# A hybrid transformer block on one core: the low part of K as one zero-padded 128-row tile per key head

## The chip, the cores and the metric

The kernel runs on one core of one Trainium2 chip, as one program in one launch. The metric is the device time of that program in microseconds, from the first to the last instruction that the device runs. Smaller is better. Inputs, weights and constant tables come from the chip's memory; the output of the last layer goes back to it.

## The reference

Two layers of a block that mixes 512 tokens `x` (width 1024) with 256 context tokens `ctx`. In each layer three branches run side by side (attention, a Fourier mixer, a long convolution called Hyena), then an output projection, then a feed-forward part with a short convolution. What matters here is the attention:

```python
kc = rmsnorm(pc_kv[..., :KV_W].reshape(B, C, N_KV_HEADS, HEAD_DIM), g_k[i])
q = rope2d(rmsnorm(px[..., Q0:K0].reshape(B, L, N_Q_HEADS, HEAD_DIM), g_q[i]), ang_r, ang_c)
k = rope2d(rmsnorm(px[..., K0:V0].reshape(B, L, N_KV_HEADS, HEAD_DIM), g_k[i]), ang_r, ang_c)
k_all = jnp.concatenate([kc, k], axis=1)          # 256 + 512 = 768 keys
s = jnp.einsum('bqhgd,bkhd->bhgqk', q, k).astype(jnp.float32) * (HEAD_DIM ** -0.5)
p = jax.nn.softmax(s, axis=-1).astype(v.dtype)
attn_x = blocked_attention(q.reshape(B, L, N_KV_HEADS, GQA_GROUP, HEAD_DIM), k_all, v_all)
```

There are 8 query heads and 2 key heads of 64 channels, so 4 query heads share a key head. In the first layer the context attends to itself as well (256 queries, 256 keys); in the last layer only `x` is computed.

## The kernel before

All products must be as exact as float32, but TensorE is fed with a reduced float type (`F32R`). So every operand is split into a high and a low part of 12 bits each, and a product is a sum of several products of parts. For most products these are three matmuls (`mm3`, lines 196 to 198): high by high, high by low, low by high.

Scores do the same with the parts stacked on partitions. The operand `Q` of one query head is a tile of 128 partitions: 64 rows hold q's high part, the other 64 its low part. For heads of key head 0 the high part is in rows 0 to 63, for heads of key head 1 in rows 64 to 127. `KD_[kv]` ("KDup") holds K's high part twice, in both halves of the partitions; one matmul over 128 rows gives (q high + q low) by K high. The third term, q high by K low, comes from the tile `KL_` ("KLo"): one tile for both key heads, with K's low part of head 0 in rows 0 to 63 and of head 1 in rows 64 to 127. That matmul reads 64 rows of `Q` and 64 rows of `KLo` (the slice `k64`), and adds to the same PSUM range.

A score tile is 128 queries by 768 keys, in a PSUM tile `pw` (there are two). It is written in two ranges of 512 and 256 columns, each with a product of KDup and a product of KLo, in this order: KDup 512 (line 966), KLo 512 (967), KDup 256 (966), KLo 256 (967). Then VectorE takes the negative maximum of each row (`nmax`, line 969), ScalarE the exponential into a tile `p` (973). There are 8 heads by 4 tiles of queries, so 32 score tiles in a layer, 64 in all. `attention` runs them ahead of the rest: a head has six steps, one for each 128 keys. A step transposes four blocks of `p` on TensorE (1018), splits the result into `pT` (ScalarE copies the high part, line 181; VectorE subtracts, line 182), and multiplies `pT` with V two steps later (1005). The first four of a head's six steps also issue a score tile of the next head. After the sixth step follow the sums of the exponentials, spread over partitions by eight small matmuls (1010), and the scaling (1090 to 1092). `attention_small` does the same for the context in the first layer, with score tiles of 256 columns (1050 and 1051), two for each of 8 heads.

KDup and KLo are filled by `post_k`: for each 128 keys a transpose (620), then copies of 64 partitions out of PSUM, two into KDup (ScalarE line 624, VectorE 625) and one into KLo (ScalarE, 626).

Tiles with the tag `M` (128 x 1024 float32 each) share 27 buffers; KDup, KLo, V, Q, p, pT, the normed operands `h` and most others are of this kind. A tile gets a buffer that is free, and its first writer waits for the last reader of the buffer's tile before.

The order of the work on each engine is not that of the code. A scheduler in the framework plays the program on a model of the engines, gives out buffers, and writes one queue for each engine; each queue is then run in its order. Beside the main line of code there are fillers (generators that are pumped while the main line would wait). SyncE's queue issues most loads, and GpSimd's (POOL) some: tables for the transforms (`dft`, `fd`), and the spilled operand `h` of the context (line 451).

Of the kernel before, what the change touches and what calls it, by code (L numbers as in the profile page):

```python
# [15 lines left out]
DRAM = bass.MemoryType.DRAM  # L16

P = 128
# [6 lines left out]
NKV = 2  # L25
# [10 lines left out]
# columns of the per-channel pack  # L36
# [9 lines left out]
def f32(ap):  # L46
    return ap.bitcast(F32)
# [6 lines left out]
# weights of products in the order of emission  # L54
# [14 lines left out]
class Net:  # L69
# [13 lines left out]
    # ---- order of emission: a main line, and fillers for the times in which it waits  # L83
# [48 lines left out]
    def go(self, name, gen, bg=0.0):  # L132
        """the main line; bg: share of fillers run beside it"""
        self.phase(name, gen)
        owed = 0.0
        for c, w in gen:
            self.now += c
            if w > 0:
                self.pump(w)
            owed += c * bg  # L140
            while owed > 0:
                f = self.ready()
                if f is None:
                    break
                t = self.now
                self.step(f)
                owed -= max(self.now - t, 0.05)
                self.now = t
            owed = min(owed, 1.0)
            self.phase(name, gen)  # L150

    # ---- tiles
# [25 lines left out]
    # ---- exact split into two parts of 12 bits  # L178
# [21 lines left out]
    # ---- 1/sqrt(sum / n + eps) of sums of n squares, by Newton steps; n a power of 4  # L200
# [18 lines left out]
    def rstd(self, ss):  # L219
        """1/sqrt of a mean square from the sums of two halves: the root, its inverse, and a Newton step"""  # L220
# [20 lines left out]
    # ---- constants  # L241
# [28 lines left out]
    # ---- modulation: block b (512 columns) of layer l  # L270
# [20 lines left out]
    def mod_chan(self, l, which, out, ahead=None):  # L291
        """which 0: norm before the mixer, 1: before the FFN."""
# [39 lines left out]
    # ---- norm of a token-major tile, transposed to channels on partitions, modulated, split  # L332
    def norm_diag(self, x, n):
        """the scale of a token on a diagonal, to be applied by the transposing product; n: where the result goes"""
# [8 lines left out]
    def turn(self, ps, n, b):  # L343
        """a half of a token tile, channels on partitions"""
# [26 lines left out]
    def norm_tile(self, st, t, n, AB, el=None, dve=4):  # L371
# [4 lines left out]
        if t == 0:  # L376
            # by 256 tokens, so that the first half of them can be read before the rest is written
# [20 lines left out]
    def norm_tile7(self, st, t, n, AB):  # L398
        """the seven left operands of Winograd's form, by halves of the tokens and of the channels"""
# [41 lines left out]
    def keep_h(self, st):  # L441
        """the operands of the next layer, kept in DRAM"""
# [19 lines left out]
    # ---- token-major products of 128 tokens with 512 columns of weights  # L462
    def proj_acc(self, st, name, l, h, tok_ap, ncol=512, early=0, late=None, w=None):
        """all the token tiles at once, by 256 of the contracted channels"""
# [28 lines left out]
    # ---- q: norm per head, RoPE, split, transposed  # L493
# [19 lines left out]
    def head_norm_rope(self, raw, nh, rstd, e, t, rope):  # L513
        """raw [P, nh, 64] -> normed, gained (and rotated) tile [P, nh, 64]"""
# [59 lines left out]
    # ---- k, v and the Fourier branch's input; tokens in the order even, odd  # L574
    def alloc_kv(self):
        self.KD_ = [self.M("KDup")[:, :768] for _ in range(NKV)]
        self.KL_ = self.M("KLo")[:, :768]
# [31 lines left out]
    def post_k(self, st, kraw, kss, kt0):  # L609
# [3 lines left out]
        for t in range(st.NT):  # L613
# [9 lines left out]
            for h in range(NKV):  # L623
                nc.scalar.copy(self.KD_[h][0:64, cs], pv[0:64, h])
                nc.vector.tensor_copy(self.KD_[h][64:128, cs], pv[0:64, h])
                nc.scalar.copy(self.KL_[64 * h : 64 * h + 64, cs], pv[64:128, h])
            yield 2 * CTR, 0.0

    # ---- Hyena branch: projection in channel-major form, short convolution
# [7 lines left out]
    def proj_hyena(self, l, st, late=None, parts=None, w=None):  # L637
# [32 lines left out]
        if late:  # L670
            # two at a time, by halves of the tokens as they become ready
# [23 lines left out]
    # ---- implicit filter and its spectrum, by even and odd taps  # L695
# [13 lines left out]
    def dft(self, key, st, a, ft):  # L709
        """two DFT matrices for one tile of frequencies, each (hi, lo)"""  # L710
# [58 lines left out]
    def filter_spectrum(self, l, st, keep, o):  # L769
# [3 lines left out]
        for ft in range(half):  # L773
            Kt = self.M("K", F32).rearrange("p (s q d) -> p s q d", s=2, q=2)
            for s in range(2):
# [4 lines left out]
                # Kt[:, s, 0]: at k; Kt[:, s, 1]: at T - k; s: cosine, sine part  # L780
                nc.vector.tensor_tensor(Kt[:, s, 0, :], eo[:, 0], eo[:, 1], op=ALU.add)
                nc.gpsimd.tensor_tensor(Kt[:, s, 1, :], eo[:, s], eo[:, 1 - s], op=ALU.subtract)
                if ft == 0 and s == 1:
                    # row 0 holds k = 0 and k = T; k = T / 2 apart
# [22 lines left out]
    # ---- Hyena branch: long convolution  # L807
    def hyena(self, l, st, keep):
# [50 lines left out]
        for ft in range(nf):  # L859
# [7 lines left out]
            # folded: [:, 0, 0] even cos, [:, 0, 1] odd cos, [:, 1, 0] even sin, [:, 1, 1] odd sin  # L867
# [29 lines left out]
    # ---- Fourier branch  # L897
# [56 lines left out]
    # ---- attention  # L954
    def scores(self, st, h, t):
# [8 lines left out]
        k64 = slice(64 * kv, 64 * kv + 64)  # L964
        for a, b in segs:
            nc.tensor.matmul(ps[:, a:b], Q[:, qs], self.KD_[kv][:, a:b], start=True, stop=False)
            nc.tensor.matmul(ps[:, a:b], Q[k64, qs], self.KL_[k64, a:b], start=False, stop=True)  # L967
# [65 lines left out]
    def attention_small(self, st):  # L1033
        """256 keys and queries: a head's scores, transposes and products in three steps"""
# [5 lines left out]
        for i in range(NH + 2):  # L1040
            c = 0.0
            if i < NH:
                kv = i // g
                k64 = slice(64 * kv, 64 * kv + 64)
# [3 lines left out]
                for t in range(NT):  # L1048
                    qs = slice(t * P, (t + 1) * P)
                    nc.tensor.matmul(sc[:, t], Q[:, qs], self.KD_[kv][:, 0:T], start=True, stop=False)  # L1050
                    nc.tensor.matmul(sc[:, t], Q[k64, qs], self.KL_[k64, 0:T], start=False, stop=True)
# [48 lines left out]
    # ---- residual update of a token-major tile: src + rstd * (y * G), in place of y * G  # L1100
# [13 lines left out]
    def mix_out(self, l, st, src, dst, nxt=None):  # L1114
        """output projection, then the residual update tile by tile"""
# [48 lines left out]
    def ffn_down(self, l, st, g, ms, begin, el=None, early=0, mid=None):  # L1164
        """the products of a group with w_down, added to y; after the last one, the residual update"""
# [41 lines left out]
    def ffn_c(self, l):  # L1207
        """the tokens of the context"""
        nc, st = self.nc, self.Cx
        G = 2  # L1210
# [29 lines left out]
    def ffn_x(self, l):  # L1240
        """the tokens of x alone; the first product by Winograd's form of Strassen's seven products"""
# [339 lines left out]
def _shape_constants():  # L1581
# [3 lines left out]
    for name, T in (("x", L), ("c", C)):  # L1585
# [3 lines left out]
        # Hyena: transform of length 2T, taps by parity  # L1589
# [12 lines left out]
        # [which, tile of frequencies, p, hi/lo, ...]  # L1602
        c[f"hdft_{name}"] = np.stack([tiles(m).reshape(P, 2, R, R, P).transpose(3, 0, 1, 2, 4) for m in fwd]).reshape(2, 2, R, P, 2, R, P).transpose(0, 2, 3, 1, 4, 5, 6)
        c[f"hinv_{name}"] = np.stack([tiles(fwd[j].T).transpose(2, 0, 1, 3) for j in (0, 2, 1, 3)]).reshape(2, 2, R, P, 2, H).transpose(0, 2, 3, 1, 4, 5)
        # Fourier: transform of length T, tokens by parity
# [7 lines left out]
        # Hyena filter: positions and windows  # L1613
# [41 lines left out]
def _layout(i):  # L1655
# [7 lines left out]
    # [l, block, half of its columns and of the contracted channels, p, 4, 256]  # L1663
# [37 lines left out]
```

## Time and profile before

| what | value |
|---|---|
| median of three runs | 1848.1 us (1838.39 to 1848.52) |
| span of the profiled execution, first to last instruction | 1850.3 us |
| mean granted TensorE clock in the profile | 0.952 |
| TensorE matmuls | 1718.8 us busy (93%), 10502 of them |
| TensorE weight loads | 1423.2 us (77%) |
| VectorE | 1446.4 us (78%) |
| ScalarE | 933.0 us (50%) |
| GpSimd | 693.4 us (37%) |
| mean DMA rate | 134 GB/s |

The profile gives no other time of its execution than this span; it is 2.2 us longer than the median of the runs. "Busy" is the time in which a row of that engine is under way; matmuls overlap, so two rows in succession can each be longer than the distance of their starts. PE is TensorE's matmul side, PEld its weight loads, DVE VectorE, ACT ScalarE, POOL GpSimd. A granted clock of 1.00 is full speed. In a row of the timeline the first column is the start in us, the second the duration in us; a merged row (x4) counts from the first start to the last end. In brackets stand the idle time before and what ended it.

### The profile page before, as it was taken

To read this page: it belongs to the slowest core of one execution; us is meant where nothing else is said; L and a number is where in the kernel's file an instruction comes from. 1 tells how busy PE (TensorE), PEld (TensorE's weight loads), DVE (VectorE), ACT (ScalarE), POOL (GpSimd) and SP (SyncE) were. 2 spreads that over 40 slices of the span, in tenths; PEclk is the share of its full clock that TensorE was granted. 3 is DMA by queue.
4 is the path that set the end of the run, shared out by engine and by line. 5 is a ranking of instruction groups with operands and counts; after the bars stand their busy time and mean duration, and the time that the engine had idled before them with its cause. 6 is when DMAs were issued, how large, how long until landed. Compare 5 with 4: busy or idle time off the path is not lost. (4 is left out here: it accounts for less than half of the span.)

```text
span 1850.3 us, 27827 instructions
## 1 busy us (share of the span) xinstructions
PE 1718.8 (93%) x10502; PEld 1423.2 (77%) x10502; DVE 1446.4 (78%) x2324; ACT 933.0 (50%) x1737; POOL 693.4 (37%) x511
## 2 busy tenths in 40 slices
PE   5899988999999998999999997998999789999997
PEld 2677865667788897878989886786678678989996
DVE  5789777567576689889898988486675976999997
ACT  2633344456574454556555556335563454545554
POOL 3344231000032447665554646021001446555552
PEclk9899999889999998999999999997799789999999
DMA  9224368500577652332342367542002253232322
GB/s 370 92 61 147 106 216 286 178 1 25 192 243 247 215 176 77 103 114 81 103 140 89 105 232 284 206 127 80 0 15 89 96 167 114 81 114 92 115 69 114
DMA packets 70002, 248.00 MB, mean 134 GB/s; under 512 B 8111, under 2 KB 9647, under 8 KB 69868
## 3 DMA queue, kind: packets, MB, share of 16 engines
q1 hardware_dynamic: 60716, 215.54, 34.4%
q0 software_dynamic: 9152, 30.68, 5.3%
q8 instruction: 83, 1.36, 0.3%
q14 instruction: 51, 0.42, 0.1%
HBM read 232.03 MB, written 14.16 MB: 133 GB/s over the span
## 5 line engine op out<-in xcount | busy, mean ns | idle before, releaser
L196 PE MATMUL pn<-h,Wh 128*128 128x256 f32 x1328 | 378.0, 287 | 8.0 <-ACT h L181 2.3
L198 PE MATMUL pn<-h,Wl 128*128 128x256 f32 x1328 | 374.3, 285 | 11.1 <-DVE Wl L182 11.1
L197 PE MATMUL pn<-h,Wh 128*128 128x256 f32 x1328 | 375.8, 284 | 1.9 <-POOL h L182 1.9
L196 PEld LDWEIGHTS pn<-h,Wh 128*128 128x128 f32 x1328 | 254.9, 193 | 20.2 <-issue 4.3
L198 PEld LDWEIGHTS pn<-h,Wl 128*128 128x128 f32 x1328 | 253.6, 192 | 16.0 <-DVE Wl L182 13.4
L197 PEld LDWEIGHTS pn<-h,Wh 128*128 128x128 f32 x1328 | 255.4, 192 | 6.3 <-POOL h L182 2.1
L181 ACT CAST Wh<-Wr 128x1024 fp32r<-128x1024 f32 x118 | 122.7, 1049 | 136.2 <-PE pn L197 46.5
L1275 POOL TENSOR_TENSOR tt<-r,r 128x512 f32<-128x512 f32 x44 | 75.9, 1724 | 270.7 <-DMA r<-w_up 243.4
L182 DVE TENSOR_TENSOR Wl<-Wr,Wh 128x1024 fp32r<-128x1024 f32 x89 | 130.3, 1472 | 50.8 <-ACT Wh L181 43.5
L196 PE MATMUL pw<-Wh,gT 128*128 128x512 f32 x352 | 137.1, 402 | 8.8 <-ACT gT L181 3.9
L197 PE MATMUL pw<-Wl,gT 128*128 128x512 f32 x352 | 138.6, 397 | 1.9 <-DVE Wl L182 1.9
L198 PE MATMUL pw<-Wh,gT 128*128 128x512 f32 x352 | 138.3, 398 | 1.8 <-DVE gT L182 1.8
L181 ACT CAST Wh<-tt 128x1024 fp32r<-128x1024 f32 x88 | 90.8, 1048 | 85.8 <-PE pn L197 43.6
L182 DVE TENSOR_TENSOR Wl<-tt,Wh 128x1024 fp32r<-128x1024 f32 x88 | 122.4, 1410 | 11.3 <-ACT Wh L181 8.4
L1334 POOL TENSOR_TENSOR ft<-ft,ft 128x512 f32<-128x512 f32 x44 | 70.6, 1603 | 133.9 <-DVE ft L635 90.7
L182 POOL TENSOR_TENSOR h<-tf,h 128x256 fp32r<-128x256 f32 (+1 forms) x40 | 38.0, 967 | 215.6 <-ACT h L181 214.2
L1201 DVE TENSOR_TENSOR y<-y,pw 128x1024 f32<-128x1024 f32 x82 | 99.3, 1214 | 22.0 <-PE pw L198 21.9
L969 DVE TENSOR_REDUCE nmax<-pw 128x1 f32<-128x768 f32 x64 | 61.1, 957 | 58.5 <-PE pw L967 58.5
L182 POOL TENSOR_TENSOR Wl<-Wr,Wh 128x1024 fp32r<-128x1024 f32 x29 | 73.1, 2526 | 58.4 <-ACT Wh L181 57.8
L1277 POOL TENSOR_TENSOR tt<-r,tt 128x512 f32<-128x512 f32 x44 | 74.8, 1699 | 50.8 <-DVE Wl L182 50.8
L181 ACT CAST pT<-pn 128x512 fp32r<-128x512 f32 x104 | 60.2, 585 | 64.2 <-PE pn L1018 61.9
L196 PE MATMUL pw<-h,Wh 128*128 128x256 f32 (+1 forms) x224 | 77.9, 348 | 12.4 <-ACT h L181 3.1
(360 smaller groups left out, 4795.7 us busy)
## 6 DMA issues: line engine op xcount, KB each, us to landing
wm<-w_mod SPq DMA_DIRECT2D x96, 512.0 KB, 5.3
r<-w_up SPq DMA_DIRECT2D x90, 512.0 KB, 3.6
Wr<-w_down SPq DMA_DIRECT2D x66, 512.0 KB, 3.7
L<-w_up SPq DMA_DIRECT2D x44, 512.0 KB, 4.6
Wr<-w_out SPq DMA_DIRECT2D x24, 512.0 KB, 3.5
Wr<-w_in_t SPq DMA_DIRECT2D x16, 512.0 KB, 4.2
dft<-hdft_x POOLq DMA_DIRECT2D x16, 512.0 KB, 4.4
Wr<-w_in_c SPq DMA_DIRECT2D x12, 512.0 KB, 3.4
```

What stands on the lines that cost most here:

```text
L181: r = nc.scalar.copy(hi, src)
L182: (el or nc.vector).tensor_tensor(lo, src, f32(hi), op=ALU.subtract)
L196: nc.tensor.matmul(ps, l[0], r[0], start=first, stop=False, **kw)
L197: nc.tensor.matmul(ps, l[0], r[1], start=False, stop=False, **kw)
L198: nc.tensor.matmul(ps, l[1], r[0], start=False, stop=last, **kw)
L969: nc.vector.tensor_reduce(nm, ps[:, :NK], axis=AX.X, op=ALU.max, negate=True)
L1201: nc.vector.tensor_tensor(y, y, acc[t], op=ALU.add)
L1275: te.tensor_tensor(half(t13, 0), half(r[1], 0), half(r[0], 0), op=ALU.subtract)
L1277: te.tensor_tensor(half(t24, 0), half(r[1], 1), half(t13, 0), op=ALU.subtract)
L1334: nc.gpsimd.tensor_tensor(o[0], o[0], o[1], op=ALU.mult)
```

## The change

Each key head gets a KLo tile of its own, of all 128 partitions. K's low part stands in 64 of its rows, where it meets q's high part; the other 64 rows, which meet q's low part, are set to zero by GpSimd when the tiles are allocated. The product with KLo then takes all 128 rows of `Q` and of `KLo`, so it has the same shape as the product with KDup. Further hunks of the diff only take comment lines out.

```diff
     def alloc_kv(self):
         self.KD_ = [self.M("KDup")[:, :768] for _ in range(NKV)]
-        self.KL_ = self.M("KLo")[:, :768]
+        self.KL_ = [self.M("KLo")[:, :768] for _ in range(NKV)]
+        for h in range(NKV):
+
+            self.nc.gpsimd.memset(f32(self.KL_[h][64 - 64 * h : 128 - 64 * h]), 0.0)
         self.V_ = [self.M("V")[:, :768].rearrange("p (t c) -> p t c", c=P) for _ in range(NKV)]
...
                 nc.vector.tensor_copy(self.KD_[h][64:128, cs], pv[0:64, h])
-                nc.scalar.copy(self.KL_[64 * h : 64 * h + 64, cs], pv[64:128, h])
+                nc.scalar.copy(self.KL_[h][64 * h : 64 * h + 64, cs], pv[64:128, h])
...
-        k64 = slice(64 * kv, 64 * kv + 64)
         for a, b in segs:
             nc.tensor.matmul(ps[:, a:b], Q[:, qs], self.KD_[kv][:, a:b], start=True, stop=False)
-            nc.tensor.matmul(ps[:, a:b], Q[k64, qs], self.KL_[k64, a:b], start=False, stop=True)
+            nc.tensor.matmul(ps[:, a:b], Q[:, qs], self.KL_[kv][:, a:b], start=False, stop=True)
...
-                k64 = slice(64 * kv, 64 * kv + 64)
...
                     nc.tensor.matmul(sc[:, t], Q[:, qs], self.KD_[kv][:, 0:T], start=True, stop=False)
-                    nc.tensor.matmul(sc[:, t], Q[k64, qs], self.KL_[k64, 0:T], start=False, stop=True)
+                    nc.tensor.matmul(sc[:, t], Q[:, qs], self.KL_[kv][:, 0:T], start=False, stop=True)
```

The scheduler places the new instructions, and some others move. Lines of the changed kernel are 3 higher behind `alloc_kv`, then 2, then 1.

GpSimd's queue in the first layer, where the context's keys are about to be projected. `fsd` and `taps` belong to the implicit filter of the Hyena branch, `fd` is a table of the Fourier branch. Before:

```order
L754 TENSOR_TENSOR fsd_1690<-dec_1687 128x256
L922 DMA fd_1869<-fdft_c 128x512
L754 TENSOR_TENSOR fsd_1750<-dec_1745 128x256
L751 TENSOR_TENSOR taps_1318<-taps_1318,fab_1747 128x512
L754 TENSOR_TENSOR fsd_1836<-dec_1831 128x256
```

The same place of the changed kernel:

```order
L757 TENSOR_TENSOR fsd_1693<-dec_1690 128x256
L580 MEMSET KLo_1654 64x768
L580 MEMSET KLo_1655 64x768
L925 DMA fd_1872<-fdft_c 128x512
L757 TENSOR_TENSOR fsd_1753<-dec_1748 128x256
L754 TENSOR_TENSOR taps_1318<-taps_1318,fab_1750 128x512
```

Two memsets of 64 rows by 768 columns stand ahead of a table's load; the work behind them keeps its order.

GpSimd's queue at the end of the first layer, where the context's operand `h` is fetched for the second layer's keys. `ft` is a gate of the feed-forward part, `y` its result. Before:

```order
L1334 TENSOR_TENSOR ft_10788<-ft_10788,ft_10789 128x512
L1334 TENSOR_TENSOR ft_10899<-ft_10899,ft_10900 128x512
L451 DMA h_10920<-spill_h 128x1024
L451 DMA h_10921<-spill_h 128x1024
L451 DMA h_10922<-spill_h 128x1024
L451 DMA h_10923<-spill_h 128x1024
L1197 TENSOR_TENSOR y_7559<-y_7559,G_5542 128x512
```

The same place of the changed kernel:

```order
L1335 TENSOR_TENSOR ft_10791<-ft_10791,ft_10792 128x512
L1335 TENSOR_TENSOR ft_10902<-ft_10902,ft_10903 128x512
L580 MEMSET KLo_10920 64x768
L580 MEMSET KLo_10921 64x768
L451 DMA h_10926<-spill_h 128x1024
L451 DMA h_10927<-spill_h 128x1024
L451 DMA h_10928<-spill_h 128x1024
L451 DMA h_10929<-spill_h 128x1024
L1198 TENSOR_TENSOR y_7562<-y_7562,G_5545 128x512
```

The memsets stand ahead of the four loads of `h`.

TensorE's queue in the first head of the first layer's attention, at a step that issues a score tile. Before:

```order
L1005 MATMUL pn_3464<-pT_3417,V_1655 128x512 x2
L1018 MATMUL pn_3467<-ident,p_3371 128x128
L1018 MATMUL pn_3467<-ident,p_3381 128x128
L1018 MATMUL pn_3467<-ident,p_3390 128x128
L1018 MATMUL pn_3467<-ident,p_3399 128x128
L966 MATMUL pw_3454<-KDup_1652,Q_951 128x512
L967 MATMUL pw_3454<-KLo_1654,Q_951 128x512
L966 MATMUL pw_3454<-KDup_1652,Q_951 128x256
L967 MATMUL pw_3454<-KLo_1654,Q_951 128x256
```

The same place of the changed kernel:

```order
L1007 MATMUL pn_3467<-pT_3420,V_1658 128x512 x2
L1020 MATMUL pn_3470<-ident,p_3374 128x128
L968 MATMUL pw_3457<-KDup_1652,Q_951 128x512
L969 MATMUL pw_3457<-KLo_1654,Q_951 128x512
L968 MATMUL pw_3457<-KDup_1652,Q_951 128x256
L969 MATMUL pw_3457<-KLo_1654,Q_951 128x256
L1020 MATMUL pn_3470<-ident,p_3384 128x128
L1020 MATMUL pn_3470<-ident,p_3393 128x128
L1020 MATMUL pn_3470<-ident,p_3402 128x128
```

Three transposes moved behind the score tile; apart from this the queue of the two attentions of `x` keeps its order, as it does on VectorE and ScalarE. Outside, the queues differ mainly in two stretches: around the first layer's projections of K and V, and from the end of the first layer's feed-forward part to the second layer's attention. There whole runs of matmuls of two accumulation groups are interleaved in another way.

## Prediction

> **What bounds the kernel now.** I read the page first (which engine is full), then the change's own lines, then the timeline around them, then busy time and granted clock by stretches.
>
> ```profile
> PE 1718.8 (93%) x10502; PEld 1423.2 (77%) x10502; DVE 1446.4 (78%) x2324; ACT 933.0 (50%) x1737; POOL 693.4 (37%) x511
> ```
>
> TensorE is the engine to look at, but 93% is an average, and overlapping rows count as busy while the array may be waiting. The products that the change touches:
>
> ```profile
> L967 PE MATMUL pw<-KLo,Q x128: 379/492/792, 316.8 to 1380.0; 64*128 64x512 f32 x64, 64*128 64x256 f32 x64
> L1051 PE MATMUL pn<-KLo,Q x16: 378/380/385, 246.0 to 302.4; 64*128 64x256 f32 x16
> ```
>
> They are 144 of 10502 matmuls. "64*128 64x512" says that they contract over 64 rows. What they cost shows in the distance of starts. First a stream of full-height products of 512 and 256 columns, then one whole score tile:
>
> ```profile
> 341.50 0.28 PE L196 MATMUL pn<-dft,Yh 128*128 128x256 f32 x1
> 341.62 0.28 PE L197 MATMUL pn<-dft,Yh 128*128 128x256 f32 x1
> ...
> 347.12 0.39 PE L196 MATMUL pn<-Wh,mx 128*128 128x512 f32 x1
> 347.36 0.40 PE L197 MATMUL pn<-Wl,mx 128*128 128x512 f32 x1
> ...
> 349.20 0.50 PE L966 MATMUL pw<-KDup,Q 128*128 128x512 f32 x1
> 349.63 0.49 PE L967 MATMUL pw<-KLo,Q 64*128 64x512 f32 x1
> 350.06 0.39 PE L966 MATMUL pw<-KDup,Q 128*128 128x256 f32 x1
> 350.37 0.38 PE L967 MATMUL pw<-KLo,Q 64*128 64x256 f32 x1
> 350.68 0.55 PE L1018 MATMUL pn<-ident,p 128*128 128x128 f32 x3
> ```
>
> In the stream a product of 512 columns takes 0.235 us from start to start (347.12 to 347.36) and one of 256 takes 0.12. In the score tile they take 0.43 and 0.31, whichever height they have. The whole tile takes 350.68 - 349.20 = 1.48 us, where 2 x 0.235 + 2 x 0.12 = 0.71 would do. The weight loads show the reason:
>
> ```profile
> 347.36 0.19 PEld L198 LDWEIGHTS pn<-Wh,mx 128*128 128x128 f32 x1
> ...
> 349.63 0.18 PEld L967 LDWEIGHTS pw<-KLo,Q 64*128 64x128 f32 x1 [0.24 <-issue]
> ```
>
> Between products of one height, the load for the next starts beside the running matmul (347.36, under the matmul of L197). Between heights it starts only with its own matmul (349.63), after an idle time that nothing but issue explains: 0.19 us more for each of the four products. So a score tile has four changes of height at about 0.19 us.
>
> Is TensorE what the attention waits for? By stretches (us, then busy time of PE, PEld, DVE, ACT, POOL, clock, DMA share, GB/s):
>
> ```profile
> 380.00:384.00 4.00, 4.00 (x11) 0.50 0.00 0
> 384.00:388.00 4.00, 4.00 (x19) 0.78 0.00 0
> ...
> 388.00:446.00 58.00, 58.00 (x287) 40.15 (x287) 43.51 (x63) 36.35 (x72) 0.00 (x0) 1.00 0.00 1
> ...
> 1284.00:1316.00 32.00, 32.00 (x77) 19.02 (x77) 12.84 (x18) 11.39 (x25) 0.00 (x0) 0.50 0.00 0
> ```
>
> (The first two show PE alone.) In the attention of `x` no transfer runs, GpSimd is idle, VectorE is busy three quarters of the time, TensorE without a gap. It is TensorE's stage. And its first head runs at **half the granted clock**, about 32 us in each layer.
>
> **Part 1: the first head, at half clock.**
>
> ```profile
> 353.73 0.79 PE L966 MATMUL pw<-KDup,Q 128*128 128x512 f32 x1 [2.50 <-ACT p L973]
> ...
> 375.27 0.78 PE L966 MATMUL pw<-KDup,Q 128*128 128x512 f32 x1
> ...
> 377.72 1.22 PE L1005 MATMUL pn<-pT,V 128*128 128x512 f32 x2
> 378.74 1.05 PE L1018 MATMUL pn<-ident,p 128*128 128x128 f32 x4
> 379.44 0.78 PE L966 MATMUL pw<-KDup,Q 128*128 128x512 f32 x1
> ...
> 385.97 0.47 PE L966 MATMUL pw<-KDup,Q 128*128 128x512 f32 x1
> ...
> 1283.29 0.79 PE L966 MATMUL pw<-KDup,Q 128*128 128x512 f32 x1 [2.31 <-ACT p L973]
> ...
> 1318.18 0.48 PE L966 MATMUL pw<-KDup,Q 128*128 128x512 f32 x1
> ```
>
> TensorE first waits 2.5 us for an exponential, whose own delay lies on ScalarE; that wait stays, so 353.73 and 1283.29 stay, and I expect the clock to fall as before. Then a step takes 379.44 - 375.27 = 4.17 us: score tile 2.45, two products with V 1.02, four transposes 0.70. At half clock the score tile without changes of height takes 2 x 0.71 = 1.42, the step 3.14.
>
> Before the steps come score tiles alone, four in layer 0 and five in layer 1, over two PSUM buffers. There the ring counts: score, maximum, exponential, then the buffer is free.
>
> ```profile
> L969 DVE TENSOR_REDUCE nmax<-pw x64: 935/958/959, 319.2 to 1380.5; 128x1 f32<-128x768 f32 x64
> ...
> L973 ACT ACTIVATE p<-pw,nmax x64: 891/902/911, 341.9 to 1381.6; 128x768 f32<-128x768 f32 x64
> L973 ACT ACTIVATION_READ_ACCUMULATOR p<-pw,nmax x64: 192/201/205, 342.7 to 1382.4; 128x1 f32 x64
> ...
> L182 DVE TENSOR_TENSOR pT<-pn,pT x29: 676/691/693, 389.0 to 443.9; 128x512 fp32r<-128x512 f32 x29
> ```
>
> (1.42 + 0.96 + 1.10) / 2 = 1.74 us a tile. Layer 0: 353.73 + 4 x 1.74 + 1.72 (V and transposes) = 362.4 for the fifth tile. Then four steps and the tail, which takes 385.97 - (379.44 + 2.45) = 4.1 now.
>
> Does the clock come back earlier? Now it returns only at about 386, behind a tail in which no score tile stands. In a step now, array work (1.42 + two products 0.94 + four transposes of some 0.5, an estimate from the rows above) fills 2.9 of 4.17 us, 69%; after the change 2.9 of 3.14, over 90%, which is like the tail. So I take it to return after one step. Layer 0: 362.4 + 3.14 + 3 steps at 2.0 (VectorE needs 0.96 + 0.69 in each, TensorE 1.5) + a tail of 2.2 = 373.8, **12.2 us** earlier. Layer 1 by the same sum: 1283.29 + 5 x 1.74 + 1.72 + 3.14 + 6.0 + 2.2 = 1305.0, **13.2 us** earlier. Should it stay at half for the whole head: 362.4 + 4 x 3.14 + 4.1 = 379.1 (6.9 us), and in layer 1 by the same sum 7.8 us.
>
> [...]
>
> **Part 2: five heads at full clock.**
>
> ```profile
> 397.27 1.05 PE L1010 MATMUL pn<-ident,den 128*128 128x128 f32 x8
> ...
> 445.87 1.05 PE L1010 MATMUL pn<-ident,den 128*128 128x128 f32 x8
> ...
> 453.75 1.05 PE L1010 MATMUL pn<-ident,den 128*128 128x128 f32 x8
> ...
> 458.91 1.05 PE L1010 MATMUL pn<-ident,den 128*128 128x128 f32 x8
> ```
>
> Line 1010 closes a head: (445.87 - 397.27) / 4 = 12.15 us each. Four score tiles give back 4 x 0.77 = 3.1, so TensorE needs 9.05. VectorE is then as late: 43.51 us in 58 is 9.1 a head. The last head, without score tiles, takes 458.91 - 453.75 = 5.16, below its VectorE rows (eight of 0.69 are 5.5, overlapping at the ends), so such a stage can run at VectorE's pace. With two equal engines and two PSUM buffers I take 9.6. That is 2.55 x 5 = 12.7, and 0.7 for one more tile: **13.4 us** a layer. Bounds: 3.1 a head (16.2 a layer) if no engine waits for another; 1.0 (5.4) if the ring of two buffers takes the rest.
>
> **Part 3: the context's attention.** 16 products of 256 columns, and 16 of KDup beside them, each 0.31 where 0.12 would do: 16 x 0.38 = 6.1 us at most; that stretch is shared with fillers that wait for transfers, so nothing at least. I take 2.
>
> **Part 4: memsets, buffers, order.** 64 rows by 768 columns on GpSimd is not in the trace. From below it may cost next to nothing; from above I take the row of 512 columns with two inputs, 1.5 times: 1.9 us.
>
> ```profile
> 195.59 0.58 POOL L922 DMA_DIRECT2D fd<-fdft_c  x1 [6.56 <-DVE dec L747]
> 196.20 0.75 POOL L754 TENSOR_TENSOR fsd<-dec 128x256 f32<-128x256 f32 x1
> 196.90 1.29 POOL L751 TENSOR_TENSOR taps<-taps,fab 128x512 f32<-128x512 f32 x1
> ...
> 1100.43 2.18 POOL L451 DMA_DIRECT2D h<-spill_h  x4
> ...
> L196 PE MATMUL pw<-M,h x16: 278/338/415, 1130.6 to 1143.2; 128*128 128x256 f32 x16
> ```
>
> In layer 0 two memsets (up to 3.9 us) fall into 6.56 us in which GpSimd waited. In layer 1 they hold the four loads of `h`, issued from 1100.43 and read from 1130.6: hidden by that distance. I take 0; uncovered it would be 4 us a layer. The second KLo tile takes one of 27 buffers until its head's keys are done; the queues of the attention kept their order, and the buffers that its p and pT tiles wait for were last read about as many instructions ahead as before. I take 0. The new interleaving outside the attention may give or take; waits there are short, so 6 us either way is my estimate, and 0 the value.
>
> **Sum.** 12.2 + 13.2 + 2 x 13.4 + 2 = 54 us. The profiled span, 1850.3, lies 2.2 above the median of the runs, and the profile shows no more of its time around it; the saving goes off the median: 1848 - 54 = **1794 us**.
>
> **Rivals.**
> 1. *The clock stays at half through the first head.* For: in the old trace 32 us of gapless rows did not raise it. Against: 69% of array work then, over 90% now. 6.9 + 7.8 + 26.8 + 2 = 44: **1804**.
> 2. *The two PSUM buffers take back most of Part 2* (1.0 a head), with or without Part 1's clock, and the new order costs 6: 25.4 + 10.8 - 6 = 30, or 20: **1818 to 1828**. For: VectorE and TensorE become equal. Against: the last head.
> 3. *The stall isn't from the height.* The idle would be there between any two products that share Q as weights and add to one PSUM range. Then nothing is saved: **1848**. Against: L966 after L1005 or L1018 has it only where heights change, and the products of a stream also add to one range. [...]
> [...]
>
> **How the numbers follow.** Forecast 54%, rival 1 26%, rival 2 10%, rival 3 7%, rival 4 3%. Low end: Part 2 at its full 16.2 a layer, Part 3 at 6, order 6: 25 + 32 + 6 + 6 = 69, 1779. High end: rival 2's 1828, so 10% is left out. One per cent (18 us) is about what a measurement of this kernel tells from no change. Faster by more than that: forecast, rival 1, rival 2 (its end is at the edge): 0.89; within 1%: 0.08; slower: 0.03.
>
> **What would show it.** Right: rows of KLo read 128*128; a score tile from start to start 0.71 at full clock; heads of 9 to 10 us; VectorE near 95% there; granted clock 1.00 from about 366 and 1297. Rival 1: clock 0.50 up to the first row of 1010. Rival 3: 0.43 between full-height scores. Wrong altogether: a row of `p` or `pT` that waits for buffers, a wait for the loads of `h` behind the memsets, or a slow stretch elsewhere.

## The result, and the profile after

The changed kernel takes 1785.6 us (median of 4 runs, 1783.0 to 1790.0) beside 1848.3 us for the kernel before. The ratio of the two is 0.9666, 95% interval 0.9637 to 0.9695, so 3.3% faster. The profiled execution has a span of 1783.1 us (before 1850.3) and a mean granted clock of 0.971 (before 0.952). Lines of the kernel after: score products 968 (KDup) and 969 (KLo), `nmax` 971, exponential 975, V 1007, end of a head 1012, transposes 1020.

Two lines of the page after:

```profile
PE 1639.1 (92%) x10502; PEld 1397.4 (78%) x10502; DVE 1440.1 (81%) x2324; ACT 934.9 (52%) x1737; POOL 692.3 (39%) x515
PEclk9899999999999998999999999999999899999999
```

TensorE runs the same 10502 matmuls in 80 us less busy time, and its share of the span hardly moves, 93 to 92%. That share could not have told what the change is worth. The answer of the trace on the product with KLo, and the second and third score tiles of `x` in layer 0 (the first stands alone at 313.55), first on TensorE and then on its weight loads:

```profile
L969 PE MATMUL pw<-KLo,Q x128: 278/387/628, 313.8 to 1317.0; 128*128 128x512 f32 x64, 128*128 128x256 f32 x64
```

```profile
344.33 0.39 PE L968 MATMUL pw<-KDup,Q 128*128 128x512 f32 x1
344.56 0.40 PE L969 MATMUL pw<-KLo,Q 128*128 128x512 f32 x1
344.80 0.28 PE L968 MATMUL pw<-KDup,Q 128*128 128x256 f32 x1
344.92 0.28 PE L969 MATMUL pw<-KLo,Q 128*128 128x256 f32 x1
345.04 0.40 PE L968 MATMUL pw<-KDup,Q 128*128 128x512 f32 x1
...
352.99 0.79 PE L968 MATMUL pw<-KDup,Q 128*128 128x512 f32 x1 [6.76 <-ACT p L975]
```

```profile
344.34 0.19 PEld L969 LDWEIGHTS pw<-KLo,Q 128*128 128x128 f32 x1
344.57 0.19 PEld L968 LDWEIGHTS pw<-KDup,Q 128*128 128x128 f32 x1
```

A tile takes 345.04 - 344.33 = 0.71 us where it took 1.48. The load for KLo starts at 344.34, together with the KDup product of 344.33 and not with its own of 344.56. The last row of TensorE is the price that was paid at once: the fourth tile (the expectations below call it the third) waits 6.76 us, before 2.50.

The ends of the heads (the products that spread the sums), head 1, 2, 6 and 8 of layer 0, 1, 6 and 8 of layer 1, and the start behind the wait in layer 1:

```profile
368.10 1.05 PE L1012 MATMUL pn<-ident,den 128*128 128x128 f32 x8
377.21 1.05 PE L1012 MATMUL pn<-ident,den 128*128 128x128 f32 x8
...
413.74 1.05 PE L1012 MATMUL pn<-ident,den 128*128 128x128 f32 x8
...
425.98 1.05 PE L1012 MATMUL pn<-ident,den 128*128 128x128 f32 x8
...
1253.19 0.80 PE L968 MATMUL pw<-KDup,Q 128*128 128x512 f32 x1 [2.70 <-ACT p L975]
...
1269.84 1.05 PE L1012 MATMUL pn<-ident,den 128*128 128x128 f32 x8
...
1315.49 1.05 PE L1012 MATMUL pn<-ident,den 128*128 128x128 f32 x8
...
1327.72 1.05 PE L1012 MATMUL pn<-ident,den 128*128 128x128 f32 x8
```

Busy time by stretches (us, then busy time with counts of PE, PEld, DVE, ACT, POOL, granted clock, DMA share, GB/s):

```profile
352.00:356.00 4.00, 3.01 (x10) 2.63 (x11) 1.31 (x4) 2.15 (x5) 0.00 (x0) 0.50 0.45 142
356.00:360.00 4.00, 3.40 (x18) 2.89 (x16) 3.51 (x6) 2.61 (x6) 0.00 (x0) 0.80 0.33 131
360.00:364.00 4.00, 3.99 (x25) 3.22 (x24) 3.73 (x6) 3.66 (x9) 0.00 (x0) 1.00 0.01 2
364.00:410.00 46.00, 46.00 (x303) 40.70 (x302) 44.57 (x68) 39.10 (x77) 0.00 (x0) 1.00 0.01 1
...
1258.00:1262.00 4.00, 3.31 (x18) 2.54 (x16) 2.72 (x5) 3.00 (x7) 0.00 (x0) 0.91 0.00 0
```

A mean clock of 0.80 in 356 to 360 is 0.50 for 1.6 us and 1.00 for the rest (357.40 to 357.60 reads 0.50, 357.80 to 358.20 reads 1.00), so the clock came back at 357.6, 4.6 us after the wait's end at 352.99; in layer 1 at 1258.7, 5.5 us after 1253.19. Before it came back at about 385.8 and, by the row below, 1317.6: 32 and 34 us after. In the steady heads VectorE is now busy 44.57 of 46 us, 97%.

```profile
1316.00:1320.00 4.00, 4.00 (x20) 3.06 (x19) 1.74 (x4) 2.16 (x4) 0.00 (x0) 0.80 0.01 4
```

Ends of heads before the change: the first of layer 0, and the first and the last of layer 1.

```profile
384.62 1.59 PE L1010 MATMUL pn<-ident,den 128*128 128x128 f32 x8
...
1317.17 1.25 PE L1010 MATMUL pn<-ident,den 128*128 128x128 f32 x8
...
1390.87 1.05 PE L1010 MATMUL pn<-ident,den 128*128 128x128 f32 x8
```

**Where the 67.2 us of span went** (before minus after):

- From the wait's end to the end of the first head: 384.62 - 353.73 = 30.9 became 368.10 - 352.99 = 15.1 in layer 0, 33.9 became 16.7 in layer 1: 15.8 + 17.2 us.
- From there to the end of the eighth head: 458.91 - 384.62 = 74.3 became 57.9; in layer 1 (last ends 1390.87 and 1327.72) 73.7 became 57.9: 16.4 + 15.8 us.
- All the rest: 2.0 us. Of it 0.7 lies ahead of the fourth tile of layer 0, 2.8 are lost between the two attentions, and 4.0 won behind the second.

### The profile page after: what moved, and what is told of

Same layout as the page of the kernel before. It is cut to its first block, busy times and chain, and to the rows that moved or that the text cites. A ratio compares the mean times of both kernels' runs of the same rounds, so it can differ in the third digit from the quotient of the medians.

```text
span 1783.1 us, 27842 instructions
## 1 busy us (share of the span) xinstructions
PE 1639.1 (92%) x10502; PEld 1397.4 (78%) x10502; DVE 1440.1 (81%) x2324; ACT 934.9 (52%) x1737; POOL 692.3 (39%) x515
## 5 line engine op out<-in xcount | busy, mean ns | idle before, releaser
L283 PE MATMUL pn<-wm,cpad 128*32 128x256 f32 x768 | 67.6, 411 | 19.7 <-DMA wm<-w_mod 19.3
L636 ACT ACTIVATE ft<-C,vec 128x512 f32<-128x512 f32 x88 | 68.7, 811 | 32.1 <-DVE C L1325 25.7
```

What stands on the lines that cost most here:

```text
L283: nc.tensor.matmul(ps[32 * g : 32 * g + 32, cs], self.cpad[:, q % 2 * 4 + g, :], w[:, g, :], start=q % 2 == 0, stop=q % 2 == 1, skip_group ...
L636: nc.scalar.activation(dst, ps, AF.Identity, scale=w1, bias=b)
```

## The experiments

Beside them the kernel before took 1848.9 to 1849.8 us. The half clock "after the wait" is read from the stretches as above. In the traces before and after the change every stretch at 0.50, apart from the one at the program's end, lasts a whole multiple of 3.41 us (in layer 0 6.8 us after the change, 350.8 to 357.6, and 34.1 before it, 351.6 to 385.7). The half clocks of layer 0 in the other kernels of the table, read from stretches of 4 us, fit this step too (6.9 us in the grouped order, 23.9 with the small 64-row products). So I compare the half clocks of two kernels only to within some 3.4 us.

| kernel | changes of height in a score tile | head at full clock, us | half clock after the wait, layer 0 and 1, us | median, us |
|---|---|---|---|---|
| before | 4 | 12.15 | 32, 34 | 1849 |
| after | 0 | 9.13 | 4.6, 5.5 | 1785.6 |
| grouped order (e1) | 2 | 10.57 | 5.5, 16 | 1826.2 |
| first head on 64 rows (e2) | 4, then 0 | 9.14 | 33, 37 | 1820.5 |
| two tiles alone (e4) | 4 | 12.15 | 19, 36 | 1854.2 |
| all score products on 64 rows (e5) | 2 | 10.57 | 27, 29 | 1817.3 |
| small 64-row products added (e9) | 4 | 12.33 | 20, 19 | 1843.2 |
| small full products added (e10) | 0 | 9.92 | 6.0, 5.5 | 1799.7 |
| everything on 64 rows (e11) | 0 | (half clock) | 87, 85 | 1947.7, one run |

**The grouped order.** Theory: a change of height costs 0.19 us. Rival: a 64-row product is slow by itself.

```diff
         for a, b in segs:
             nc.tensor.matmul(ps[:, a:b], Q[:, qs], self.KD_[kv][:, a:b], start=True, stop=False)
+        for a, b in segs:
             nc.tensor.matmul(ps[:, a:b], Q[k64, qs], self.KL_[k64, a:b], start=False, stop=True)
```

> The kernel before, with the four score products of a tile in another order: both KDup products, then both 64-row KLo products, so that the row height changes twice a tile instead of four times. Theory (each change of height costs about 0.19 us, four a tile make the 0.77 us between 1.48 and 0.71): a tile at full clock takes 1.09 to 1.11 us, a head in the steady stretch 12.15 - 4 x 0.38 = 10.6 us, and the kernel about 2 x 6 x 1.55 = 19 us less than 1848, 1829 (1800 if the clock also comes back in the first head). Rival (a 64-row product is slow by itself, wherever it stands): a tile stays at 1.48, a head at 12.15, the kernel at 1848.

1826.2 us, ratio 0.9872 (0.9849 to 0.9894). One tile of the steady stretch (merged rows, 512 and 256 columns) and two ends of heads:

```profile
370.69 1.05 PE L1011 MATMUL pn<-ident,den 128*128 128x128 f32 x8
...
386.60 0.59 PE L966 MATMUL pw<-KDup,Q 128*128 128x512 f32 x2
387.13 0.61 PE L968 MATMUL pw<-KLo,Q 64*128 64x512 f32 x2
387.67 0.50 PE L1006 MATMUL pn<-pT,V 128*128 128x512 f32 x1
...
412.98 1.05 PE L1011 MATMUL pn<-ident,den 128*128 128x128 f32 x8
```

The same products in another order: the tile takes 387.67 - 386.60 = 1.07 us and the head (412.98 - 370.69) / 4 = 10.57. Half of the changes gone, half of the stall gone. The rival is out.

That the kernel came near the expected 1829 us is luck. That number left the first head at half clock; 1800 was to hold if the clock came back, and it did. In the profile the two attentions won 41 us, of the 65 that the whole change won there: from the wait's end to the end of the eighth head 83.0 us instead of 105.2 in layer 0, and 88.3 instead of 107.6 in layer 1. But the part behind the second attention, from the end of its eighth head, took 472.0 us instead of 459.4. There the queues of ScalarE, VectorE and GpSimd stand in another order than before; no run shows that this alone is the cause.

**The first head alone on 64 rows.** Part 1 of the prediction undone, Part 2 kept.

```diff
-            nc.tensor.matmul(ps[:, a:b], Q[:, qs], self.KL_[kv][:, a:b], start=False, stop=True)
+            r = slice(64 * kv, 64 * kv + 64) if st is self.X and (h < 2 or h == 2 and t < 3) else slice(0, P)
+            nc.tensor.matmul(ps[:, a:b], Q[r, qs], self.KL_[kv][r, a:b], start=False, stop=True)
```

> The kernel after, with 64-row KLo products again in the first eleven score tiles of x's attention only (the same two tiles of SBUF, the same memsets). Theory (the stalls of the mixed heights hold the clock down after the wait): the clock of the first head is 0.50 for about 32 us again, the five following heads keep their 9.1 us, and of the 66 us the two first heads give back 16.5 + 17.2 = 33, so about 1818. Rival (the clock comes back by itself after a few us, and the old half clock had another cause): clock 1.00 from about 357 and 1258, and only 11 x 0.77 us a layer is lost, 17 us in all, about 1802.

1820.5 us, ratio 0.9828 (0.9807 to 0.9849):

```profile
356.00:384.00 28.00, 28.00 (x70) 17.01 (x70) 13.47 (x20) 10.30 (x21) 0.00 (x0) 0.50 0.05 19
384.00:388.00 4.00, 4.00 (x18) 3.61 (x18) 1.48 (x3) 2.16 (x4) 0.00 (x0) 0.56 0.00 0
388.00:434.00 46.00, 46.00 (x304) 40.78 (x303) 44.29 (x66) 38.66 (x75) 0.00 (x0) 1.00 0.00 1
```

Half clock until 387.5, then heads as fast as after the change. The 35 us that eleven tiles a layer give back are over half of the gain, and half clock is what makes them so dear: 11 x 2 x 0.77 would be 17.

**The context's attention alone on 64 rows** (Part 3 undone).

```diff
-                    nc.tensor.matmul(sc[:, t], Q[:, qs], self.KL_[kv][:, 0:T], start=False, stop=True)
+                    r = slice(64 * kv, 64 * kv + 64)
+                    nc.tensor.matmul(sc[:, t], Q[r, qs], self.KL_[kv][r, 0:T], start=False, stop=True)
```

> The kernel after, with 64-row KLo products again in the context's attention only (256 keys). Theory: its products lie before the wait for w_out and the casts behind it, which takes the lead back (the start of the third score tile moved by only 0.7 us), so 0 to 1 us slower, 1785 to 1787. Rival (Part 3 of the prediction reaches the end): about 2 us slower, or up to 6 by its upper bound, 1788 to 1792.

1788.4 us, ratio 0.9669 (0.9654 to 0.9683): no difference that the runs can tell from 0.9666. The median itself lies in the rival's range, so the run doesn't decide between the two. In this one profile the fourth tile starts 1.5 us later than after the change (354.53, behind a wait of 7.28).

**The tiles and memsets alone**: the edit of the last run, and in `scores`:

```diff
-            nc.tensor.matmul(ps[:, a:b], Q[:, qs], self.KL_[kv][:, a:b], start=False, stop=True)
+            r = slice(64 * kv, 64 * kv + 64)
+            nc.tensor.matmul(ps[:, a:b], Q[r, qs], self.KL_[kv][r, a:b], start=False, stop=True)
```

> The kernel after, with two KLo tiles and their memsets but every KLo product on 64 rows as before. Theory (the whole gain is in the products' height): 1848 within 6 us, heads 12.15 us, clock 0.50 in the first head. Rival (the second tile or the scheduler's new order made part of the gain): more than 8 us below 1848.

1854.2 us, ratio 1.0028 (1.0017 to 1.0039): 5 us slower than before. Tiles, memsets and the new order bring nothing; they cost about 0.3%. In the one profile the stretch between the two attentions is 5.3 us longer than before (829.7 us beside 824.4) and the fourth tile starts 3.0 us later. The first head of layer 0 is 5.1 us shorter, because its half clock ended 19 us after the wait; that was not expected.

**All score products on 64 rows**, in the kernel before:

```diff
-            nc.tensor.matmul(ps[:, a:b], Q[:, qs], self.KD_[kv][:, a:b], start=True, stop=False)
+            nc.tensor.matmul(ps[:, a:b], Q[k64, qs], self.KD_[kv][k64, a:b], start=True, stop=False)
```

> The kernel before, with the KDup products of x's attention also on 64 rows only (the row half of their key head; the product of K's high part with one part of q is left out). Four 64-row products stand in a tile instead of two, but the height changes only twice, at the tile's ends. Theory (the change costs 0.19 us, the height nothing): the tile's time with its two changes is that of the grouped order, 1.07 to 1.10 us, a head 10.6 us, the kernel about 1826. Rival (each 64-row product is 0.38 us slower than a full one): a tile 0.71 + 4 x 0.38 = 2.2 us, a head about 15 us, the kernel 35 us or more above 1848. On the clock of the first head: 1.00 within about 14 us of the wait's end if the stalls hold it down (as in the grouped order), 0.50 for 25 us or more if it is the rows that stand idle.

1817.3 us, ratio 0.9845 (0.9817 to 0.9873).

```profile
388.45 1.05 PE L1010 MATMUL pn<-ident,den 128*128 128x128 f32 x8
...
420.15 1.05 PE L1010 MATMUL pn<-ident,den 128*128 128x128 f32 x8
```

```profile
352.00:376.00 24.00, 24.00 (x69) 16.83 (x68) 14.47 (x21) 11.52 (x24) 0.00 (x0) 0.50 0.16 64
376.00:380.00 4.00, 4.00 (x20) 3.45 (x19) 1.78 (x4) 2.16 (x4) 0.00 (x0) 0.69 0.00 0
```

A head takes (420.15 - 388.45) / 3 = 10.57, to the hundredth that of the grouped order, with twice as many 64-row products. So at full clock the height costs nothing and the change of height does. The half clock, with the same stalls as in the grouped order, lasts longer (27 and 29 us beside 5.5 and 16). Stalls alone do not explain it. The two attentions together take 14 us longer than in the grouped order; that this kernel is still the faster one goes with the 12.5 us that the grouped order loses behind them.

**The change of height by itself**: in the kernel after, one small product of 32 columns more behind each pair, on 64 rows; and as a control the same on all 128 rows (`r = slice(0, P)`).

```diff
             nc.tensor.matmul(ps[:, a:b], Q[:, qs], self.KL_[kv][:, a:b], start=False, stop=True)
+            if st is self.X:
+                r = slice(64 * kv, 64 * kv + 64)
+                c = 768 + a // 8
+                nc.tensor.matmul(ps[:, c : c + 32], Q[r, qs], self.KL_[kv][r, a : a + 32], start=True, stop=True)
```

> The kernel after, with one more product behind each pair of score products of x's attention: 64 rows by 32 columns, into columns of the same PSUM tile that nobody reads. The height changes four times a tile again, as before the change, and the 64-row work is next to nothing. Theory on the pace (the change of height is the cost, 0.18 to 0.19 us each): a head at full clock 9.13 + 4 x (4 x 0.18 + 2 x 0.03) = 12.2 to 12.4 us. Rival on the pace (64-row work is slow in proportion to its columns): 9.2 to 9.5 us. On the clock of the first head: 0.50 for 25 us or more if the stalls alone hold it down, as before the change; 5 to 15 us as in the grouped order if it goes by the rows at work, averaged over the stalls too. In all 1825 to 1850.

> The same with the two small products on all 128 rows, so that no height changes: what the small products cost by themselves. Both theories: 0.03 to 0.06 us each, a head 9.1 to 9.6 us, the clock back after about 4 us, 1785 to 1792 in all. If a head comes out near 12 us instead, it is not the height but the small products, and the run before this one says nothing.

1843.2 us (ratio 0.9977, 0.9959 to 0.9994) and 1799.7 us (0.9732, 0.9703 to 0.9762). Ends of heads with the 64-row products, then with the full ones:

```profile
380.62 1.05 PE L1016 MATMUL pn<-ident,den 128*128 128x128 f32 x8
...
417.60 1.06 PE L1016 MATMUL pn<-ident,den 128*128 128x128 f32 x8
```

```profile
395.69 1.05 PE L1016 MATMUL pn<-ident,den 128*128 128x128 f32 x8
...
425.44 1.05 PE L1016 MATMUL pn<-ident,den 128*128 128x128 f32 x8
```

(417.60 - 380.62) / 3 = 12.33 us a head beside (425.44 - 395.69) / 3 = 9.92. The control was dearer than expected, 0.10 us for a small product, where 0.03 to 0.06 was my estimate, which no run shows. Against it 16 changes in a head cost 2.41, 0.15 us each; between the kernels before and after it is 3.02 / 16 = 0.19, and in the grouped order 1.44 / 8 = 0.18. Of the 58 us that come back (1843.2 beside 1785.6), 14 are the small products' own (1799.7 beside 1785.6); the other 43.5 go with the height. The half clock, 20 and 19 us, lies between what the two theories gave (25 or more, 5 to 15).

**Everything on 64 rows**: the scores as in all score products on 64 rows, and the rest of the attention likewise. No height changes within it, but half of the rows idle.

```diff
-                nc.tensor.transpose(pt[:, t * P : (t + 1) * P], st.p[h, t][:, kt * P : (kt + 1) * P], self.ident)
+                nc.tensor.matmul(pt[:, t * P : (t + 1) * P], st.p[h, t][k64, kt * P : (kt + 1) * P], self.ident[k64], start=True, stop=True)
...
-                nc.tensor.matmul(acc[h], v, pT[:, e], start=kt == 0 and e == 0, stop=kt == NKT - 1 and e == 1)
+                nc.tensor.matmul(acc[h], v[k64], pT[k64, e], start=kt == 0 and e == 0, stop=kt == NKT - 1 and e == 1)
```

> The kernel before, with every TensorE product of x's attention on 64 rows: scores, transposes (as plain products with a half of the unit matrix), the products with V and the sums for the denominators. It leaves out the other half of each contraction, and no height changes within the attention. On the clock: back at 1.00 within about 5 us of the wait if only the stalls of the changes hold it down; 0.50 through the whole attention, some 100 us, if the rows that stand idle hold it down. The pace of a tile follows the clock, 0.71 us at 1.00 and about 1.45 at 0.50, and so does the time: about 1790 to 1800, or 1860 and more.

1947.7 us in its one run.

```profile
356.00:432.00 76.00, 76.00 (x312) 69.56 (x312) 38.27 (x55) 30.58 (x60) 0.00 (x0) 0.50 0.05 15
```

76 us without a gap and without a change of height, at half clock. It came back only at about 441, where heads of the two key heads alternate and products on the upper and the lower rows run side by side (two of 512 columns start at 437.63 and 437.78, 0.15 us apart, where one key head's start at 407.38 and 407.95, 0.57 apart). It fell again at 462, after 20 us of work on 64 rows without a gap, and stayed at 0.50 until 509.7. So changes of height are not needed to hold the clock down. But the run differs in one thing more: as plain products the transposes come as eight rows a step and not four.

```profile
373.25 0.77 PE L966 MATMUL pw<-KDup,Q 64*128 64x512 f32 x1
...
375.53 1.91 PE L1020 MATMUL pn<-ident,p 64*128 64x128 f32 x8
377.09 0.77 PE L966 MATMUL pw<-KDup,Q 64*128 64x512 f32 x1
```

They take 1.56 us (375.53 to 377.09) of a step of 3.84, and whether they bear on the clock like the rest is not shown. That idle rows lengthen the half clock shows better in all score products on 64 rows beside the grouped order (27 and 29 us beside 5.5 and 16), with the same number of changes. Stalls and idle rows both stood in the first head before the change.

**What the longer wait costs.** After the change, ScalarE's queue ahead of the exponential that the fourth tile waits for:

```profile
349.58 1.04 ACT L181 CAST Wh<-Wr 128x1024 fp32r<-128x1024 f32 x1 [2.02 <-DMA Wr<-w_out]
350.65 1.28 ACT L975 ACT_TABLE_LOAD   x1
351.94 0.90 ACT L975 ACTIVATE p<-pw,nmax 128x768 f32<-128x768 f32 x1
```

A cast for the output projection, which comes after the attention, waits for its weights, and the exponential stands behind it, with a table load of 1.28 us between. Three runs tried to win this back: the casts behind the first exponentials (`lt` is true for `w_out` of `x` in layer 0), products that nobody reads in the wait, and both (with 14 and 11 products).

```diff
+        if (h, t) == (0, 3):
+            self.ex = ex.ins
...
+                    with self.tc.issue_after(self.ex) if lt else nullcontext():
+                        w[q] = self.load_w(src, [P, n, ncol], el=nc.gpsimd if lt else None, tag="M" if q < early else None, raw="Wr")
```

```diff
         yield ahead(2), Z["at0"]
+        wm = self.pn()
+        for i in range(28 if self.lay == 0 else 11):
+            nc.tensor.matmul(wm, st.Q[0][:, 0, 0:P], self.KL_[0][:, 256:768], start=True, stop=True)
```

> The kernel after, with the casts of x's w_out weights in layer 0 queued on ScalarE behind the exponentials of the first score tiles, and their second parts taken on GpSimd. Theory (the 6.76 us wait of the third score tile is the casts' wait for w_out): that tile starts at about 349.5 instead of 352.99, and the kernel takes 2 to 4 us less than 1785. Rival (VectorE's or the clock's return sets the head, or the later weights delay the output projection): 1785 within 2 us, or more.

> The kernel after, with full-height products into a tile that nobody reads (28 in layer 0, 11 in layer 1) in TensorE's wait before the third score tile. Theory (the idle wait is what drops the clock to 0.50, and full-height work holds it): the clock reads 1.00 through 344 to 364 and 1249 to 1262, a lead-in tile takes 0.71 us, and the kernel 2 to 4 us less than 1785. Rival (the drop has another cause, or the lead-in is set by ScalarE and VectorE): 0.50 again at 353 in spite of them, or 1.00 without a gain, 1785 within 2 us.

> Both of these together (14 and 11 products in the waits). If the two gains are independent, they add up: 4 to 8 us less than 1785. If the pace of the lead-in is that of ScalarE and VectorE, no more than the larger of the two.

1785.2, 1785.4 and 1783.8 us, ratios 0.9655 (0.9633 to 0.9676), 0.9658 (0.9639 to 0.9677) and 0.9652 (0.9632 to 0.9672): no gain that can be told. The casts behind the exponentials:

```profile
349.24 0.50 PE L971 MATMUL pw<-KDup,Q 128*128 128x512 f32 x1 [1.78 <-ACT p L978]
...
353.08 0.48 PE L971 MATMUL pw<-KDup,Q 128*128 128x512 f32 x1
...
355.77 0.79 PE L971 MATMUL pw<-KDup,Q 128*128 128x512 f32 x1 [1.51 <-ACT p L978]
```

Both together, by stretches:

```profile
344.00:364.00 20.00, 16.14 (x88) 12.75 (x88) 13.85 (x23) 16.12 (x30) 9.05 (x4) 1.00 0.35 112
```

The wait is 1.78 us instead of 6.76, but the casts now stand between the exponentials of the tiles that follow, and TensorE waits there. With the products that nobody reads, layer 1 keeps a clock of 1.00 throughout its attention (every stretch of 4 us from 1238 to 1266 reads 1.00, and behind them, up to 1400, no single row of 512 columns is longer than 0.58 us); layer 0 falls to 0.50 at about 357 (a mean of 0.68 in 356 to 360), once they are done and TensorE waits again (1.06 us ahead of 357.09). In layer 0 these products also hold back the third tile, which after the change followed the second at once, at 345.04:

```profile
346.55 6.52 PE L999 MATMUL pn<-KLo,Q 128*128 128x512 f32 x28
352.91 0.39 PE L968 MATMUL pw<-KDup,Q 128*128 128x512 f32 x1
```

So there this run does not price the clock alone. The attention begins at another time in each profile, so the gain is read from the start of the second tile in layer 0, and of the first in layer 1, to the end of the first head. After the change that is 23.8 and 23.7 us, with the casts behind 22.8 and 23.6, with the products 24.3 and 22.2, with both 23.2 and 22.2. These gains of 1 to 2 us in all are too small for the medians to tell.

With both the clock is 1.00 all the way. At that clock TensorE idles about 4 of these 20 us, and ScalarE, with the four casts among its exponentials, is as busy as it is. So the wait had not been the only thing as late as the first head's end; the lead-in's exponentials were next.

## Why the prediction was right, and where its sizes were off

**The mechanism (four changes of height at about 0.19 us) held.** The change itself and three experiments price it at 0.15 to 0.19 us. Rival 3, that the idle isn't from the height, is out: two products that share Q and add to one range follow each other at 0.23 us after the change. Nor did a load wait for the product ahead where both had one height: the load at 344.34 starts under the product of 344.33, both on 128 rows. What TensorE does at a change of height no trace shows, only that it takes these 0.15 to 0.19 us.

**Part 1 (12.2 + 13.2) measured 15.8 + 17.2.** The step that was mis-sized is "So I take it to return after one step": it put the clock's return at about 366 and 1297, one step behind the lead-in, 12 and 14 us after the wait. It came 4.6 and 5.5 us after it, inside the lead-in. The score tiles and transposes that stand there are full-height work without stalls too, and I had costed them at 1.74 us a tile, at half clock throughout. Rival 1 (half clock through the first head) failed in the other direction. That the share of array work decides, and not that of rows, fits the runs in kind: idle rows (e5 beside e1, 27 and 29 us beside 5.5 and 16) and changes of height (e9 beside e10, 20 and 19 us beside 6.0 and 5.5) each lengthen the half clock, in rows without a gap. Rows without a gap did not bring the clock back by themselves: 76 us of them ran at 0.50 with everything on 64 rows.

**Part 2 (13.4 a layer) measured 16.4 and 15.8.** The bound taken was "9.6" a head, between 9.1 and the ring of two buffers; the heads took 9.13. The ring takes nothing: VectorE runs at 97% and TensorE without a gap, so the upper bound of 16.2 a layer was the right one. Rival 2 (1818 to 1828) is out. So is the slower kernel that was given 3%, with half clock through the whole attention: the clock reads 1.00 from 360 on.

**Part 3 (2 us) did not get through.** The second score tile of `x` started 3.5 us earlier (347.82 and 344.33), and the wait for the casts took back 2.8 of them before the fourth. The step "that wait stays, so 353.73 and 1283.29 stay" was right for the time at which it ends, 352.99, and I had then added Part 3 ahead of it all the same.

**Part 4 (0, between -6 and 6) measured about 5 us of loss** (the tiles alone). The memsets, which take 0.735 us each and not up to 1.9, keep nobody waiting that the trace shows; what remains is the order outside the attention, which differs from kernel to kernel. In that profile 5.3 us are lost between the two attentions, and with the full change 2.8; what costs them there stays open.

**The sum.** 54 us predicted, 62.7 measured by the medians, 67.2 by the two profiles. Most of the difference between the two is in the profile before. A run's time is 1.8 us longer than the span of its profile (1784.9 and 1783.1 after the change); if that held before too, the execution with the span of 1850.3 took some 4 us more than the median, and not 2.2. The terms err to one side: 7.6 us too little in Part 1, 5.4 in Part 2. That all the rest comes to 2.0 us, as large as Part 3, is luck: it is the sum of 0.7, -2.8 and 4.0 us in other places.

## What to carry to other kernels

Read the distance of starts, not the busy share: rows of 512 columns were 0.39 and 0.50 us long where their starts lay 0.235 and 0.43 us apart, and TensorE read as 92 or 93% busy with and without the stalls. A mix of 64-row and 128-row products cost 0.15 to 0.19 us at each change. Rows filled up with zeros took no time of their own here: heads with two changes a tile took 10.57 us whether eight or sixteen of their score products had 64 rows. Where products must be short in rows, put those of one height together, which needs no second tile. Here it brought 41 of the 65 us within the two attentions, and 23 of the 63 in all. And a stretch at half clock is a second cost of the same stalls: price it apart, since here the two first heads were half of the gain.

## What the runs showed that was not expected

- Work on half of the rows went on at a granted clock of 0.50 without any change of height: 76 us of 64-row products without a gap. The slower transposes of that run are not separated from it. Estimated from the rows of a step at half clock (3.14 us of work, some 0.26 a change, 64-row work counted half), the share of full-array work is at most about 50% there (87 us at half clock), 67% before (32 and 34) and with all scores on 64 rows (27 and 29), 75% with the small 64-row products (20 and 19), 76% in the grouped order (5.5 and 16), near 100% after (5). The order of the half clocks is that of these shares, but 75 and 76% lie close together for such different times, and the tiles alone, with the products of the kernel before, took 19 us in layer 0. So the place of the return also hangs on something finer, perhaps the order of a few products or where a step of 3.41 us begins. What exactly the clock goes by stays open.
- A product of 32 columns on full height costs 0.10 us of TensorE's time here, though its 32 columns at 0.235 us for 512 would take 0.015.
- A stretch of 6.76 us in which TensorE waits drops the clock from 1.00 to 0.50 (at 350.8, 4.6 us into it). With products that nobody reads in its place the clock reads 1.00 up to the wait's end, and the kernel gains nothing that the runs can tell.
